# Seven products of quarters instead of eight in the second MLP product of a streaming encoder layer

## The chip, the cores and the metric

The kernel runs on one core of one Trainium2 chip. The metric is the device time of one execution in microseconds (us), the median over runs. The core has a matrix engine (PE, with its own row PEld for the loading of stationary operands), a vector engine (DVE), an activation engine (ACT), a general engine (POOL) and a queue that issues transfers (SP). Each works through its own list of instructions in order and waits on semaphores for the others.

## The reference

One layer with two sub-layers, 512 tokens of 1024 features, all in float32. The first is a mixer (sparse attention with a top-k selection of keys, beside a convolution module), the second the squared-ReLU MLP that the change is about:

```python
x = x + gt1 * (mixed @ w_out[l])
h2 = rms_norm(x, g_norm2[l]) * (1.0 + sc2) + sh2
f = jnp.square(jax.nn.relu(h2 @ w_ff1[l])) @ w_ff2[l]      # w_ff1: 1024 x 4096, w_ff2: 4096 x 1024
x = x + gt2 * f
```

## The kernel before

**Products in three passes.** Every float32 product is made of three matmuls on operands split into a rounded high part and the rest: high times high, high times low, low times high (`mm3`). A weight tile of 128 x 512 therefore takes a cast on ACT (`wh_...`, the high part) and a subtraction (`wl_...`, the low part) on DVE or POOL; the table `ENG` names the engine for each pair of tiles (`P` for POOL, `V` for DVE). The tiles `wh` and `wl` live in rings of four buffers each, so at most four weight tiles stand ahead of PE.

**The MLP in blocks.** The 4096 hidden features are cut into four blocks of 1024 (`NB`). For one block, `ff1` makes two groups of 512 hidden features (first product, hidden features on the partitions, tokens along the moving side), applies ReLU and square on ACT, and splits the result `f` (high part by a DVE cast, low part by a POOL subtraction). `ff2` multiplies them with the block's rows of `w_ff2` (second product, 128 tokens per bank, 512 output columns) in two column halves `n` and adds the banks `y...` to an accumulator `facc` in SBUF.

**Three phases.** `PHASES` says which tokens a block is done for. `A` blocks do the first 256 tokens (`fA`, `yA`) as soon as these are through the mixer; `F` blocks do all 512 tokens (`fF`, `yF`); `B` blocks at the end do the last 256 tokens (`fB`, `yB`) for the blocks that `A` did. With `NA = 2`, blocks 0 and 1 go through `A` and `B`, and blocks 2 and 3 through `F`. In `A` and `B` the first product has a moving side of 256 tokens, in `F` of 512. After the last but one contribution the accumulator is multiplied by the gate `gt2` and added to the residual `x` on POOL; the last contribution is gated and added on DVE and stored.

**What sets the order.** All operations are recorded, and a list scheduler in the kernel (`_Plan`) places them engine by engine. An operation's urgency comes from the numbers in the table `URG`; buffers from rings are given out while it plans. All instructions are issued by one helper line, L433 in the profile of this kernel (L436 after the change), so rows are told apart by tile names. `blk` tiles are sixteen buffers of 128 x 2048 words for everything large.

The names after the change: `q...` is a quarter of the block's part of `w_ff2` (512 rows by 512 columns), `t1` a stored combination of quarters, `p1` to `p7` the seven products (two banks each), `lh`/`ll` the high and low part of a left operand (256 tokens by 512 hidden features, in two steps), `u` a partial sum that two output quarters share.

Of the kernel before, what the change touches and what calls it, by code (L numbers as in the profile page):

```python
# [18 lines left out]
P = 128  # L19
# [11 lines left out]
NEG_MASK = -1.0e30  # L31
FILLER = False
URG = dict(
    ahead_c1=837.59, ahead_iq=272.3, warm=546.0, g0=-393.95, gr=-25.32, w72=-132.21, ps72=260.94,
    start=-1047.26, glu=36.26, c0=-607.51, ik=-47.66, iq=-114.09, iqn=547.0, idx=-2.2, rel=-14.62, topk=612.37,
    c1=602.08, q=132.4, qn=717.77, k=161.16, kn=23.37, qT=215.6, v=238.29, vn=144.89, kT=270.05, tapV0=-394.95,
    tapV1=-965.11, tapV2=584.84, tapV3=12.43, tapP0=202.52, tapP1=412.49, tapP2=412.6, tapP3=-1042.96,
    sh2=117.75, sc2=780.82, gt1=-341.13, gt2=-105.75, gemv_step=23.900000000000006, ahead_x=-11.51,
    ahead=150.51, cn=119.17, pyc=38.83, oC=531.98, attn=-1100.76, sm=-209.79999999999995, pv=-37.5,
    sq=-103.80000000000004, oA=415.94, n2=537.09, ff=543.09, tapVs=33.89999999999999, tapPs=25.450000000000003,  # L40
    topks=18.800000000000004, idxs=5.0, ns=24.0, projs=6.749999999999996, cns=17.89999999999999, oCs=-0.5,
    attns=13.850000000000001, topkB=1479.47, qTB=611.37, attnB=177.79, oB=574.12, n2B=543.32,
)
ENG = dict(
    sl0B="P", sl1B="V", oAmul0="P", oAmul1="P", oAadd0="V", oAadd1="P", oBmul0="V", oBmul1="V", oBadd0="V",
    oBadd1="V", gt1="T", gt2="V", round0="T", round1="T", round2="T", round3="T", sl0="A", sl1="P", rope_q="P",
    rope_k="P", rope_iq="P", gb="P", oAadd="P", oCmul="A", oAmul="V", lo_c0="V", lo_c1="V", lo_iq="P", lo_q="P",
    lo_k="P", lo_v="P", lo_oC="P", lo_oA="P", lo_oB="P", lo_f1A="PPVV", lo_f2A="PVVV", lo_f1F="VPPP",
    lo_f2F="PVPP", lo_f1B="PVPV", lo_f2B="VVVP", h2lo0="V", h2lo1="V", aff0="A", aff1="A", mixA="P", tap0="A",
)  # L50
POOL_TAPS = (7, 7, 11, 12)
NB = 4
NA = 2
NBLK = 16
PHASES = (("A", range(NA)), ("F", range(NA, NB)), ("B", range(NA)))


# [456 lines left out]
def layer_kernel(  # L514
# [52 lines left out]
    def blk(shape, dt, name):  # L567
        return big.tile(shape, dt, tag="B", bufs=NBLK, name=name)

# [14 lines left out]
    def raw(ap):  # L584
        return ap.bitcast(F32)
# [690 lines left out]
    def x2(t):  # L1276
        return x2s[t // 2][:, t % 2, :]
# [213 lines left out]
    facc = [blk([P, 2, D], F32, f"facc{half}") for half in range(2)]  # L1491
    count = [0, 0]

    def ff1(b, g, part):
        c0 = b * 1024 + g * 512
        name = f"f{part}{b}{g}"
        hi, lo = dict(A=h2a, B=h2b, F=h2)[part]
        width = S if part == "F" else 256
        banks = [acc_bank(f"{name}_{j}") for j in range(4)]
        for k in (0, 2, 4, 6):  # L1500
            e = dict(P=pl.gpsimd, V=pl.vector)[ENG[f"lo_f1{part}"][k // 2]]
            w = split_weights(rows2(w_ff1, k, c0), f"{name}{k}", e)
            feat_major(banks, w, k, 2, hi, lo, k == 0, k == KD - 2, width)
        if part == "F":
            f = [blk([P, 4, S], F32R, f"{name}{a}") for a in range(2)]
            for j in range(4):
                r = tmp_tile(f"r{name}{j}")
                pl.scalar.activation(r, banks[j], AF.Relu)
                pl.scalar.activation(r, r, AF.Square)
                pl.vector.tensor_copy(f[0][:, j, :], r)  # L1510
                pl.gpsimd.tensor_sub(f[1][:, j, :], r, raw(f[0][:, j, :]))
            return f
        f = blk([P, 2, 4, 256], F32R, name)
        for j in (0, 2):
            r = tmp_tile(f"r{name}{j}").rearrange("p (j q) -> p j q", j=2)
            for jj in range(2):
                pl.scalar.activation(r[:, jj, :], banks[j + jj][:, :256], AF.Relu)
            pl.scalar.activation(r, r, AF.Square)
            pl.vector.tensor_copy(f[:, 0, j : j + 2, :], r)
            pl.gpsimd.tensor_sub(f[:, 1, j : j + 2, :], r, raw(f[:, 0, j : j + 2, :]))  # L1520
        return [f[:, 0], f[:, 1]]

    def ff2(b, n, part, fts):
        c0 = n * 512
        tiles = dict(A=(0, 1), B=(2, 3), F=(0, 1, 2, 3))[part]
        banks = {t: wk_bank(f"y{part}{b}{n}_{t}") for t in tiles}
        for k in (0, 2, 4, 6):
            e = dict(P=pl.gpsimd, V=pl.vector)[ENG[f"lo_f2{part}"][k // 2]]
            w = split_weights(rows2(w_ff2, b * 8 + k, c0), f"y{part}{b}{n}{k}", e)
            f = fts[k // 4]  # L1530
            for t in tiles:
                i = t if part == "F" else t % 2
                s = slice(i * P, (i + 1) * P)
                for kk in range(2):
                    j = k % 4 + kk
                    mm3(banks[t], (f[0][:, j, s], f[1][:, j, s]), w[kk], k + kk == 0, k + kk == 7)
        for t in tiles:
            a = facc[t // 2][:, t % 2, c0 : c0 + 512]
            xs = x2(t)[:, c0 : c0 + 512]
            g = gt2[:, c0 : c0 + 512]  # L1540
            m = count[t // 2]
            if m == 0:
                pl.scalar.copy(a, banks[t])
            elif m < NB - 1:
                pl.vector.tensor_add(a, banks[t], a)
            else:
                pl.vector.tensor_mul(a, banks[t], g)
                pl.vector.tensor_add(a, a, xs)
                pl.sync.dma_start(out[t * P : (t + 1) * P, c0 : c0 + 512], a)
            if m == NB - 2:  # L1550
                pl.gpsimd.tensor_mul(a, a, g)
                pl.gpsimd.tensor_add(xs, xs, a)

    for part, blocks in PHASES:
        for b in blocks:
            fts = []
            for g in range(2):
                step += 1
                pl.level = (URG["ff"] + 20 * step,)
                fts.append(ff1(b, g, part))  # L1560
            for n in range(2):
                step += 1
                pl.level = (URG["ff"] + 20 * step,)
                ff2(b, n, part, fts)
            for h in dict(A=(0,), B=(1,), F=(0, 1))[part]:
                count[h] += 1
# [53 lines left out]
```

## Time and profile before

| | us |
|---|---|
| median of 3 runs (lowest, highest) | 665.84 (665.34, 665.88) |
| the profiled execution | 665.98 |
| its span, first to last instruction | 664.1 |
| PE busy | 639.7 (96%) |
| DVE busy | 402.8 (61%) |
| POOL busy | 393.7 (59%) |
| ACT busy | 347.7 (52%) |

1.9 us of the profiled execution lie outside its span. Busy shares are means over stages with different limits; the stages in the trace are: mixer to 299 us, `A` blocks 298.9 to 394.8, `F` blocks 394.8 to 568.9, `B` blocks from 568.9 to the end. A matmul's recorded duration overlaps that of its neighbours, so the pace of a stream of them is taken from a stretch of time divided by their count. The same holds for DVE: what counts in a row of operations is the distance from start to start.

### The profile page before, as it was taken

How to read it: one execution, taken by the hardware profiler on the slowest of the kernel's cores; microseconds unless marked ns; L12 is line 12 of the kernel's file. 1: busy time of each engine (PE TensorE's matmuls, PEld its weight loads, DVE VectorE, ACT ScalarE, POOL GpSimd, SP SyncE). 2: the span in 40 equal slices, each digit the busy share in tenths (PEclk: the TensorE clock that was granted, in tenths of full speed). 3: DMA queues.
4: the chain of work that ended last, by engine and by line, in shares of the span. 5: the costliest groups of instructions: out<-in, count | busy, mean ns of one | idle time of the engine just before them, and what ended most of it. 6: DMA issues, size and time to landing. Idle time of an engine off the chain costs nothing. (4 is left out here: it accounts for less than half of the span.)

```text
span 664.1 us, 10353 instructions
## 1 busy us (share of the span) xinstructions
PE 639.7 (96%) x3654; PEld 523.0 (79%) x3654; DVE 402.8 (61%) x812; ACT 347.7 (52%) x711; POOL 393.7 (59%) x379
## 2 busy tenths in 40 slices
PE   3999999999998999999999999999999999999997
PEld 2776776878675776679989988888888888998985
DVE  4657999999999899987752641122102220465564
ACT  3327625894359855976656533342225422464552
POOL 2008936999999789633445523766466643448941
PEclk9999999999999899999999999999999999999999
DMA  9969995423031264107565563232322334555552
GB/s 292 348 207 388 368 387 198 162 64 96 33 95 36 94 221 127 32 17 224 177 200 178 190 191 112 80 96 95 125 86 84 118 85 137 159 183 179 185 186 94
DMA packets 61662, 105.09 MB, mean 158 GB/s; under 512 B 6233, under 2 KB 22825, under 8 KB 61610
## 3 DMA queue, kind: packets, MB, share of 16 engines
q1 hardware_dynamic: 61514, 104.39, 48.2%
q8 instruction: 29, 0.48, 0.3%
q14 instruction: 23, 0.19, 0.1%
q10 hardware_dynamic: 96, 0.03, 0.0%
HBM read 100.22 MB, written 2.10 MB: 154 GB/s over the span
## 5 line engine op out<-in xcount | busy, mean ns | idle before, releaser
L433 PE MATMUL yF<-wh_yF,fF 128*128 128x512 f32 x256 | 79.2, 389 | 0.0
L433 PE MATMUL fF<-h,wh_fF 128*128 128x512 f32 x256 | 78.8, 389 | 0.0
L433 DVE SCALAR_TENSOR_TENSOR run<-u,wdw,run 128x512 f32<-128x512 f32 x83 | 58.9, 748 | 0.2
L433 PEld LDWEIGHTS yF<-wh_yF,fF 128*128 128x128 f32 x256 | 48.0, 188 | 10.1
L433 PEld LDWEIGHTS fF<-h,wh_fF 128*128 128x128 f32 x256 | 48.0, 188 | 10.0
L433 POOL TENSOR_TENSOR wl_yF<-wr_yF,wh_yF 128x512 fp32r<-128x512 f32 x24 | 30.5, 1291 | 35.5 <-ACT wh_yF L433 35.5
L433 PE MATMUL fF<-h,wl_fF 128*128 128x512 f32 x128 | 49.8, 389 | 0.0
L433 PE MATMUL yF<-wl_yF,fF 128*128 128x512 f32 x128 | 49.8, 389 | 0.0
L433 ACT CAST wh_yF<-wr_yF 128x512 fp32r<-128x512 f32 x32 | 19.9, 622 | 51.5 <-PE yF L433 38.6
L433 PE MATMUL fA<-h2a,wh_fA 128*128 128x256 f32 x256 | 46.5, 284 | 0.0
L433 POOL TENSOR_TENSOR cacc<-cacc,prod 128x512 f32<-128x512 f32 x33 | 44.0, 1336 | 3.7 <-ACT prod L433 2.9
L433 POOL TENSOR_TENSOR wl_fF<-wr_fF,wh_fF 128x512 fp32r<-128x512 f32 x24 | 31.3, 1324 | 24.8 <-ACT wh_fF L433 22.1
L433 PE MATMUL fB<-h,wh_fB 128*128 128x256 f32 x256 | 45.4, 283 | 0.0
L433 ACT CAST wh_fF<-wr_fF 128x512 fp32r<-128x512 f32 x32 | 19.9, 622 | 45.4 <-PE fF L433 37.5
L433 PEld LDWEIGHTS fA<-h2a,wh_fA 128*128 128x128 f32 x256 | 40.0, 191 | 0.3
L433 PE MATMUL yA<-wh_yA,fA 128*128 128x512 f32 x128 | 39.7, 389 | 0.0
L433 PE MATMUL yB<-wh_yB,fB 128*128 128x512 f32 x128 | 39.6, 390 | 0.0
L433 PEld LDWEIGHTS fB<-h,wh_fB 128*128 128x128 f32 x256 | 39.5, 192 | 0.2
L433 PE MATMUL fA<-h2a,wl_fA 128*128 128x256 f32 x128 | 35.7, 283 | 0.0
L433 PE MATMUL fB<-h,wl_fB 128*128 128x256 f32 x128 | 34.8, 284 | 0.2 <-POOL wl_fB L433 0.2
L433 DVE CAST fF<-rfF 128x512 fp32r<-128x512 f32 x16 | 8.2, 523 | 43.9 <-ACT rfF L433 43.9
L433 DVE TENSOR_TENSOR wl_fF<-wr_fF,wh_fF 128x512 fp32r<-128x512 f32 x8 | 5.5, 693 | 48.1 <-ACT wh_fF L433 48.1
(328 smaller groups left out, 1845.4 us busy)
## 6 DMA issues: line engine op xcount, KB each, us to landing
wa_gt<-in_w_ada_dram SPq DMA_DIRECT2D x16, 512.0 KB, 9.4
wr_fA<-in_w_ff_dram SPq DMA_DIRECT2D x16, 512.0 KB, 4.1
wr_yA<-in_w_ff_dram SPq DMA_DIRECT2D x16, 512.0 KB, 3.8
wr_fF<-in_w_ff_dram SPq DMA_DIRECT2D x16, 512.0 KB, 3.8
wr_yF<-in_w_ff_dram SPq DMA_DIRECT2D x16, 512.0 KB, 3.6
wr_fB<-in_w_ff_dram SPq DMA_DIRECT2D x16, 512.0 KB, 4.1
wr_yB<-in_w_ff_dram SPq DMA_DIRECT2D x16, 512.0 KB, 3.7
ada<-in_w_ada_dram SPq DMA_DIRECT2D x12, 512.0 KB, 8.4
```

The costliest lines, as they stand in the source:

```text
L433: f(*map(real, args), **{k: real(v) for k, v in kwargs.items()})
```

## The change

For `F` blocks (`SEVEN = "F"`) the second product is done by quarters. The left side `f` (512 tokens by 1024 hidden features) and the right side (1024 by 1024) are each cut into two by two quarters, and seven products of sums and differences of quarters replace the eight plain ones. The sums of left quarters (`fsum`) are done in place on DVE, the sums of weight quarters (`wsum`) on DVE for three tiles of four and on POOL for one; `f` is kept in plain float32, and each of the seven left operands is split anew (high part on ACT, low part on DVE), as is each of the 28 weight tiles (high part on ACT, low part on DVE). Products that two output quarters share are added to both.

`NA` goes from 2 to 1: block 0 alone goes through `A` and `B`, blocks 1, 2 and 3 through `F`. Both tables are new. One more convolution tap is done by ACT and POOL in place of DVE (`POOL_TAPS`). In `B`, all low parts and the split of `f` go to DVE, and so do the gating and the addition to the residual ahead of the last contribution (`foldF`).

```diff
-    lo_k="P", lo_v="P", lo_oC="P", lo_oA="P", lo_oB="P", lo_f1A="PPVV", lo_f2A="PVVV", lo_f1F="VPPP",
-    lo_f2F="PVPP", lo_f1B="PVPV", lo_f2B="VVVP", h2lo0="V", h2lo1="V", aff0="A", aff1="A", mixA="P", tap0="A",
+    lo_k="P", lo_v="P", lo_oC="P", lo_oA="P", lo_oB="P", lo_f1A="PPVP", lo_f2A="PVPV", lo_f1F="PVPP",
+    lo_f2F="VVVP", lo_f1B="VVVV", lo_f2B="VVVV", sumF="VPVV", losF="VVVV", fsumF="V", fhiF="A", floF="V",
+    uaddF="V", foldF="V", frest="V", h2lo0="V", h2lo1="V", aff0="A", aff1="A", mixA="P", tap0="A",
 )
-POOL_TAPS = (7, 7, 11, 12)
+POOL_TAPS = (7, 8, 11, 12)
 NB = 4
-NA = 2
+NA = 1
+SEVEN = "F"
...
-    def ff1(b, g, part):
+    def ff1(b, g, part, pair=None):
...
+        if part in SEVEN:
+            f = blk([P, 4, S], F32, name) if part == "F" else pair[:, g]
+            for j in range(4):
+                pl.scalar.activation(f[:, j, :], banks[j][:, :width], AF.Relu)
+                pl.scalar.activation(f[:, j, :], f[:, j, :], AF.Square)
+            return f
...
-            pl.gpsimd.tensor_sub(f[:, 1, j : j + 2, :], r, raw(f[:, 0, j : j + 2, :]))
+            eng("frest").tensor_sub(f[:, 1, j : j + 2, :], r, raw(f[:, 0, j : j + 2, :]))
...
+    def evict(bank, t, n, m, last):
+        c0 = n * 512
+        a = facc[t // 2][:, t % 2, c0 : c0 + 512]
+        xs = x2(t)[:, c0 : c0 + 512]
+        g = gt2[:, c0 : c0 + 512]
+        if m == NB - 1 and last:
+            pl.vector.tensor_mul(a, bank, g)
+            pl.vector.tensor_add(a, a, xs)
+            pl.sync.dma_start(out[t * P : (t + 1) * P, c0 : c0 + 512], a)
+            return
+        if (t, n) not in begun:
+            pl.scalar.copy(a, bank)
+        elif bank.tile.psum:
+            pl.vector.tensor_add(a, bank, a)
+        else:
+            eng("uaddF").tensor_add(a, bank, a)
+        begun.add((t, n))
...
+    def ff2_seven(b, part, f, lev_load, start):
...
+        a11, a21 = (f[0][:, :, r * half : (r + 1) * half] for r in range(2))
+        a12, a22 = (f[1][:, :, r * half : (r + 1) * half] for r in range(2))
+        quarters = []
+        with pl.after([start]), pl.urgency(lev_load):
+            for g, n in ((0, 0), (0, 1), (1, 1), (1, 0)):
+                q = blk([P, 4, 512], F32, f"q{part}{b}{g}{n}")
+                for k in (0, 2):
+                    pl.sync.dma_start(q[:, k : k + 2, :], rows2(w_ff2, b * 8 + 4 * g + k, n * 512))
+                quarters.append(q)
+        b11, b12, b22, b21 = quarters
...
+        def product(name, l, r):
+            banks = [wk_bank(f"{name}{part}{b}_{i}") for i in range(half // P)]
+            level = pl.level[0]
+            with pl.urgency(level - URG["ahead"]):
+                ls = left(l, f"{name}{part}{b}")
+            for k in range(4):
+                with pl.urgency(level - URG["ahead"]):
+                    w = right(r, k, f"{name}{part}{b}")
+                for i, bank in enumerate(banks):
+                    s = slice(i * P, (i + 1) * P)
+                    mm3(bank, (ls[k][0][:, s], ls[k][1][:, s]), w, k == 0, k == 3)
+            return banks
...
+        for k in range(4):
+            wsum("tensor_sub", k, t1, b12, b11)
+        for k in range(4):
+            wsum("tensor_sub", k, b12, b22, b12)
+        p = product("p1", a11, b11)      # copied to u (ACT), added to output quarter 1,1
+        fsum("tensor_sub", a11, a11, a21)
+        p = product("p7", a11, b12)      # added to quarters 2,2 and 2,1
+        wsum("tensor_add", k, b11, b11, b12)
+        p = product("p2", a12, b21)      # added to quarter 1,1
+        fsum("tensor_sub", a11, a22, a11)
+        p = product("p6", a11, b11)      # added to u, and u to quarter 2,1
+        wsum("tensor_sub", k, b12, b21, b11)
+        p = product("p4", a22, b12)      # added to quarter 2,1
+        fsum("tensor_add", a21, a21, a22)
+        p = product("p5", a21, t1)       # added to u, and u to quarters 2,2 and 1,2
+        fsum("tensor_sub", a11, a12, a11)
+        p = product("p3", a11, b22)      # added to quarter 1,2
```

(The last part is shortened: levels, loops over `k` and the additions are told in words after the `#`.)

The order that the scheduler makes of it, at three places. In the names, the digits after `F` or `B` count the block, and after it the weight tile: `wl_p2F22` is the low part of the third weight tile of product `p2` in block 2, `yF30_1` the bank of tokens 128 to 255, column half 0, in block 3.

**PE, second product of an all-token block.** Before (block 3), each bank gets its matmuls tile by tile, the three passes of a tile together (`fF300` and `fF301` are the high and low part of `f`):

```order
L433 MATMUL yF30_0_5661<-wh_yF3000_5608,fF300_5474 128x512
L433 MATMUL yF30_0_5661<-wl_yF3000_5613,fF300_5474 128x512
L433 MATMUL yF30_0_5661<-wh_yF3000_5608,fF301_5480 128x512
L433 MATMUL yF30_0_5661<-wh_yF3001_5615,fF300_5474 128x512
L433 MATMUL yF30_0_5661<-wl_yF3001_5623,fF300_5474 128x512
L433 MATMUL yF30_0_5661<-wh_yF3001_5615,fF301_5480 128x512
```

After (block 2, products `p2` and `p6`):

```order
L436 MATMUL p2F2_1_5400<-wh_p2F21_5372,llp2F20_5362 128x512
L436 MATMUL p2F2_0_5390<-wh_p2F22_5383,lhp2F22_5366 128x512
L436 MATMUL p2F2_1_5400<-wh_p2F22_5383,lhp2F22_5366 128x512
L436 MATMUL p6F2_0_5422<-wh_p6F20_5407,lhp6F20_5393 128x512
L436 MATMUL p2F2_0_5390<-wl_p2F22_5413,lhp2F22_5366 128x512
L436 MATMUL p2F2_0_5390<-wh_p2F22_5383,llp2F22_5376 128x512
L436 MATMUL p2F2_1_5400<-wl_p2F22_5413,lhp2F22_5366 128x512
L436 MATMUL p2F2_1_5400<-wh_p2F22_5383,llp2F22_5376 128x512
```

The passes that need only high parts, one of them of the next product, have moved ahead of those with the low part `wl_p2F22`.

**DVE, second product of an all-token block.** Before (block 3), two low parts, two casts of `f` and the first sum out of a bank stand in a row, and this is most of what DVE has in half of a second product:

```order
L433 TENSOR_TENSOR wl_yF3020_5663<-wr_yF302_5531,wh_yF3020_5655 128x512
L433 TENSOR_TENSOR wl_yF3021_5674<-wr_yF302_5531,wh_yF3021_5667 128x512
L433 CAST fF310_5636<-rfF312_5651 128x512
L433 CAST fF310_5636<-rfF313_5671 128x512
L433 TENSOR_TENSOR facc0_4128<-yF30_0_5661,gt2_968 128x512
L433 TENSOR_TENSOR facc0_4128<-facc0_4128,x20_2963 128x512
```

After (block 2, from `p6` to `p4`):

```order
L436 TENSOR_TENSOR llp6F22_5439<-fF20_5086,lhp6F22_5428 128x512
L436 TENSOR_TENSOR facc0_4106<-p2F2_0_5390,facc0_4106 128x512
L436 TENSOR_TENSOR facc0_4106<-p2F2_1_5400,facc0_4106 128x512
L436 TENSOR_TENSOR wl_p6F21_5456<-qF200_4951,wh_p6F21_5420 128x512
L436 TENSOR_TENSOR wl_p6F22_5462<-qF200_4951,wh_p6F22_5436 128x512
L436 TENSOR_TENSOR wl_p6F23_5466<-qF200_4951,wh_p6F23_5452 128x512
L436 TENSOR_TENSOR qF201_4961<-qF210_4984,qF200_4951 128x512 x2
L436 TENSOR_TENSOR llp4F20_5480<-fF21_5252,lhp4F20_5446 128x512
L436 TENSOR_TENSOR wl_p4F20_5489<-qF201_4961,wh_p4F20_5460 128x512
L436 TENSOR_TENSOR uF2_0_5331<-p6F2_0_5422,uF2_0_5331 128x512
```

The low parts of the weights of two products are now mixed with sums out of banks, sums of weight quarters (`qF201`), splits of left operands (`ll`) and partial sums (`uF2`), without a break.

**DVE, start of the B block.** Before, after the sums out of the last `yF` banks:

```order
L433 TENSOR_TENSOR facc1_5185<-yF31_2_5838,facc1_5185 128x512
L433 TENSOR_TENSOR facc1_5185<-yF31_3_5845,facc1_5185 128x512
L433 TENSOR_TENSOR wl_fB0020_5975<-wr_fB002_5834,wh_fB0020_5960 128x512
L433 TENSOR_TENSOR wl_fB0021_5982<-wr_fB002_5834,wh_fB0021_5968 128x512
L433 TENSOR_TENSOR wl_fB0060_6043<-wr_fB006_5908,wh_fB0060_6031 128x512
L433 TENSOR_TENSOR wl_fB0061_6050<-wr_fB006_5908,wh_fB0061_6040 128x512
```

After:

```order
L436 TENSOR_TENSOR wl_fB0000_6346<-wr_fB000_5807,wh_fB0000_6335 128x512
L436 TENSOR_TENSOR facc1_4677<-uF3_0_6042,facc1_4677 128x512
L436 TENSOR_TENSOR wl_fB0001_6356<-wr_fB000_5807,wh_fB0001_6349 128x512
L436 TENSOR_TENSOR facc1_4677<-uF3_1_6053,facc1_4677 128x512
L436 TENSOR_TENSOR wl_fB0020_6368<-wr_fB002_5850,wh_fB0020_6360 128x512
L436 TENSOR_TENSOR facc0_4106<-uF3_0_6042,facc0_4106 128x512
L436 TENSOR_TENSOR facc0_4106<-uF3_1_6053,facc0_4106 128x512
L436 TENSOR_TENSOR wl_fB0021_6391<-wr_fB002_5850,wh_fB0021_6375 128x512
L436 TENSOR_TENSOR x20_2959<-x20_2959,facc0_4106 128x512
L436 TENSOR_TENSOR facc0_4106<-p2F3_1_6111,gt2_960 128x512
```

The low parts of the B block's first weights are mixed with the sums and gatings that the last block of seven products leaves behind.

More of the change, by code (lines that the diff above doesn't have):

```diff
@@ L33 @@
 URG = dict(
[L34 to L42, printed above, removed]
+    ahead_c1=1124.25, ahead_iq=270.95, warm=-302.25, g0=-2.77, gr=-946.01, w72=-374.86, ps72=142.64,
@@ new lines @@
+    start=-1336.17, glu=220.87, c0=-516.25, ik=-128.98, iq=-203.0, iqn=802.64, idx=-944.18, rel=-72.55,
+    topk=217.54, c1=807.1, q=89.88, qn=475.39, k=121.19, kn=-274.6, qT=191.77, v=220.03, vn=-196.25, kT=57.55,
+    tapV0=-112.18, tapV1=-903.31, tapV2=532.94, tapV3=-44.08, tapP0=20.16, tapP1=709.96, tapP2=-50.45,
+    tapP3=-907.8, sh2=71.07, sc2=1160.76, gt1=-376.43, gt2=-91.51, gemv_step=14.099999999999998, ahead_x=40.59,
+    ahead=106.98, cn=131.33, pyc=-292.14, oC=416.69, attn=-947.53, sm=-318.99999999999983,
@@ L43 @@
+    pv=-17.900000000000034, sq=-106.10000000000007, oA=368.14, n2=542.37, ff=604.64, tapVs=30.900000000000002,
+    tapPs=80.45000000000006, topks=17.30000000000001, idxs=8.65, ns=27.050000000000008, projs=6.999999999999994,
+    cns=29.400000000000027, oCs=-0.2, evict=475.23, usum=80.52, attns=32.800000000000054, topkB=1787.89,
+    qTB=389.63, attnB=230.88, oB=621.61, n2B=662.17,
 )
 ENG = dict(
-    sl0B="P", sl1B="V", oAmul0="P", oAmul1="P", oAadd0="V", oAadd1="P", oBmul0="V", oBmul1="V", oBadd0="V",
+    sl0B="P", sl1B="V", oAmul0="V", oAmul1="P", oAadd0="P", oAadd1="P", oBmul0="V", oBmul1="P", oBadd0="P",
@@ L1492, in layer_kernel @@
     count = [0, 0]
-    def ff1(b, g, part):
+    seven_last = [h for h, part in enumerate("FB") if part in SEVEN]
+    begun = set()
+    def ff1(b, g, part, pair=None):
         c0 = b * 1024 + g * 512
@@ L1552, in ff2 @@
                 pl.gpsimd.tensor_add(xs, xs, a)
+    def evict(bank, t, n, m, last):
[14 more added lines that the diff above has]
+            eng("uaddF").tensor_add(a, bank, a)
+        begun.add((t, n))
@@ L1556, in layer_kernel @@
             fts = []
+            pair = blk([P, 2, 4, 256], F32, f"f{part}{b}") if part in SEVEN and part != "F" else None
+            mark = len(pl.ops)
             for g in range(2):
@@ L1559, in layer_kernel @@
                 pl.level = (URG["ff"] + 20 * step,)
-                fts.append(ff1(b, g, part))
+                fts.append(ff1(b, g, part, pair))
+            start = next(op for op in pl.ops[mark:] if op.engine == "tensor")
+            if part in SEVEN:
+                lev_load = pl.level[0] - 20
+                step += 1
+                pl.level = (URG["ff"] + 20 * step,)
+                step += 1
+                ff2_seven(b, part, fts, lev_load, start)
+                for h in dict(A=(0,), B=(1,), F=(0, 1))[part]:
+                    count[h] += 1
+                continue
             for n in range(2):
```

85 lines of the change are left out of this document (added).

## Prediction

> **What bounds the kernel now.** I read the page's busy shares and slices first, then busy times by stage, then the matmul pace, then the rows of DVE, the engine that gets the new work.
>
> ```profile
> span 664.1 us, 10353 instructions
> PE 639.7 (96%) x3654; PEld 523.0 (79%) x3654; DVE 402.8 (61%) x812; ACT 347.7 (52%) x711; POOL 393.7 (59%) x379
> PE   3999999999998999999999999999999999999997
> DVE  4657999999999899987752641122102220465564
> ```
>
> PE is full from the second slice on; DVE is full until slice 17 (282 us) and nearly idle in slices 25 to 34. The same by stage (busy us of PE, PEld, DVE, ACT, POOL, with counts; then clock, transfers):
>
> ```profile
> 195.00:250.00 55.00, 50.85 (x262) 38.35 (x261) 50.96 (x158) 44.74 (x131) 47.09 (x57) 0.97 0.33 106
> 250.00:299.00 49.00, 45.99 (x260) 34.04 (x259) 44.84 (x121) 36.69 (x101) 31.30 (x34) 1.00 0.19 60
> 325.00:395.00 70.00, 70.00 (x415) 62.51 (x415) 36.58 (x48) 42.03 (x81) 30.18 (x22) 1.00 0.60 188
> 395.00:482.00 87.00, 87.00 (x385) 72.03 (x385) 15.39 (x21) 30.53 (x52) 49.47 (x39) 1.00 0.33 103
> 482.00:569.00 87.00, 87.00 (x386) 72.03 (x385) 16.65 (x25) 29.39 (x50) 45.71 (x36) 1.00 0.32 99
> 438.40:482.00 43.60, 43.60 (x194) 36.12 (x193) 9.96 (x12) 13.03 (x23) 24.75 (x20) 1.00 0.32 100
> ```
>
> From 325 to 569 us PE has no gap at all: it alone sets that stage, and what it is spared there is gained, as long as the others keep up. DVE does 12 operations in a second product (last row). Mixer stages lose 4.15 and 3.01 us of PE, together 7.2.
>
> **The change part by part.** *Fewer matmuls.* Two rows: the 512-wide matmuls of one `F` block, and a stretch of a `B` block's first product, 256 wide.
>
> ```profile
> 395.00:482.00 87.00, 86.95 (x384) 72.03 (x385) 4.10 (x8) 4.77 (x8) 10.30 (x8) 1.00 0.33 103
> 569.00:592.00 23.00, 23.00 (x193) 22.96 (x192) 9.88 (x14) 12.83 (x26) 10.19 (x8) 1.00 0.59 192
> ```
>
> A 512-wide matmul costs 86.95/384 = 0.2264 us, a 256-wide one 23.00/193 = 0.119. A second product falls from 192 matmuls to 7 x 24 = 168, in three blocks: 72 x 0.2264 = 16.3 us. Block 1 goes from two halves (2 x 192 x 0.119 = 45.8) to one `F` product (192 x 0.2264 = 43.5): 2.3 us; its second product in halves has as many matmuls as whole. PE is spared **18.6 us**. The same block also loads its 16 weight pieces once instead of twice, worth nothing, since no PE wait on them shows above.
>
> *What DVE gets.* Counted in the order, from the third weight tile of `p1` (the first that must wait for `ff1` to release a buffer) to the last tile of `p3`, DVE has 58, 59 and 65 operations in the three blocks: 26 low parts of weights, 11 of left operands, 4 sums of left and 5 of weight quarters, 12 to 14 sums out of banks or of `u`, and in the last block 5 gatings and final additions. PE takes 168 x 0.2264 = 38.0 us for this. All are 128 x 512; the rows that price them:
>
> ```profile
> 319.91 1.28 DVE L433 TENSOR_TENSOR wl_fA<-wr_fA,wh_fA 128x512 fp32r<-128x512 f32 x2
> 321.11 1.28 DVE L433 TENSOR_TENSOR x<-x,xr 128x512 f32<-128x512 f32 x2
> 322.32 1.28 DVE L433 TENSOR_TENSOR wl_fA<-wr_fA,wh_fA 128x512 fp32r<-128x512 f32 x2
> 647.33 0.69 DVE L433 TENSOR_TENSOR facc<-yB,gt 128x512 f32<-128x512 f32 x1
> 648.06 0.69 DVE L433 TENSOR_TENSOR facc<-facc,x 128x512 f32<-128x512 f32 x1
> 648.69 0.69 DVE L433 TENSOR_TENSOR facc<-yB,gt 128x512 f32<-128x512 f32 x1
> 649.30 1.29 DVE L433 TENSOR_TENSOR wl_yB<-wr_yB,wh_yB 128x512 fp32r<-128x512 f32 x2
> ```
>
> Each is recorded with 0.69 us, but they start closer: two every 1.20 to 1.21 (0.60 each) when independent, 0.61 to 0.63 beside a bank, 0.73 where one needs the one just before. With five to seven of the last kind among some 60 I take **0.62** on average, with 0.60 and 0.69 as ends.
>
> Such an operation is late when 0.7 us (the cast on ACT ahead of the first) plus 0.62 x its place exceeds the time at which PE comes to it. Seven products are 5.43 us each, one weight tile 1.36. In block 1 the latest is the second tile of `p3`, place 56: 0.7 + 34.7 against 6 x 5.43 + 1.36 = 33.9, late by 1.5. In block 2 it is the second tile of `p4`, place 40: 25.5 against 23.1, late by 2.4. In block 3, again the second tile of `p3`, place 63: 39.8 against 33.9, late by 5.9. Whatever is late is PE time, since PE's list holds the next block's matmuls only behind `p3`. Sum **9.8** (at 0.60: 0.4 + 1.6 + 4.6 = 6.6; at 0.69, where block 2 is latest at place 57: 5.4 + 6.1 + 10.3 = 21.8). What is queued behind on DVE is the next tiles' low parts, which is why lateness carries over from product to product.
>
> In the `B` block all low parts are DVE's now, behind sums and gatings: the second tile of the seventh pair has place 33 after the last tile of `p3`, so 20.5 us against 1.36 + 6 x 24 x 0.119 + 3 x 0.119 = 18.9: late by **1.6** (0.9 to 3.9).
>
> *POOL beside DVE.* One sum of weight quarters of four stays on POOL. What a POOL operation does to DVE:
>
> ```profile
> 595.21 2.38 DVE L433 TENSOR_TENSOR wl_yB<-wr_yB,wh_yB 128x512 fp32r<-128x512 f32 x2
> 595.36 1.67 POOL L433 TENSOR_TENSOR fB<-rfB,fB 128x512 fp32r<-128x512 f32 x1 [1.56 <-DVE fB L433]
> ```
>
> Two operations take 2.38 instead of 1.28 when one of POOL's falls between: 1.1 us. Within a second product POOL has two; the first falls where DVE waits for ACT anyway, the second (`b12` during `p7`) where DVE has no slack. So 1.1 per block, **3.3** in all (0 if it falls in a gap, 6.6 if both count).
>
> *ACT.* Per second product 28 casts of weights and 14 of left operands. Two casts take 1.30 us, 0.69 apart:
>
> ```profile
> 645.29 1.30 ACT L433 CAST wh_yB<-wr_yB 128x512 fp32r<-128x512 f32 x2 [1.42 <-PE yB L433]
> ```
>
> 42 x 0.69 = 29, and with copies to `u` and the last squares of `ff1` some 33 of 38 us: it fits, and costs nothing by itself. If ACT slipped, DVE's low parts would be late next, by the same amount.
>
> *Transfers.* Quarters come in 8 pieces of 512 KB per block, as before, but are released only when the block's first matmul starts. That lets SP hold later pieces of `w_ff1` behind them; a piece lands in 3.6 to 3.8 us and the pieces behind are needed over 27 us later (half of 43.5 plus 5.4), so nothing:
>
> ```profile
> wr_fF<-in_w_ff_dram SPq DMA_DIRECT2D x16, 512.0 KB, 3.8
> wr_yF<-in_w_ff_dram SPq DMA_DIRECT2D x16, 512.0 KB, 3.6
> ```
>
> *One block ahead, not two.* `F` needs the second half's normalised tokens. When these are ready, and when `F` starts:
>
> ```profile
> L433 DVE TENSOR_TENSOR h<-ht,h x4: 692/694/1668, 309.4 to 330.9; 128x512 fp32r<-128x512 f32 x4
> L433 PE MATMUL fF<-h,wh_fF x256: 389/389/389, 395.0 to 525.2; 128*128 128x512 f32 x128
> ```
>
> Ready at 331.6. `F` moves forward by one `A` block, 192 x 0.119 + 96 x 0.2264 = 44.6 us, to 350.4. That leaves 18.8 us of cover: nothing. If it were gone, PE would wait for these tokens microsecond for microsecond.
>
> *The mixer's new order and the tap taken from DVE.* The same matmuls, another order. The bounds are the 7.2 us of gaps above: at best they close, at worst they grow by about half, 3. I take 0, as no row prefers a side.
>
> The sum: -18.6 + 9.8 + 1.6 + 3.3 = **-3.9**. The profiled execution took 665.98 (1.9 outside its span, 0.1 over the median of 665.84), so **662.1 us**.
>
> VectorE: DVE Perf Modes, a page of the Trainium skill, says under "The DRAIN you can't avoid" that the next DVE operation starts only once the pipe has emptied behind the one before. If that meant a full 0.69 us for each, the sum would come to the slower side. The trace does not bear it out for independent operations: six in a row start 0.60 apart.
>
> **The rivals.** (1) *DVE takes its full recorded time*, because its operations wait one by one for casts, banks or their predecessors. For it: 0.73 between dependent ones, and the order alternates such kinds. Against: runs at 0.60. At 0.69 the lateness is 21.8 + 3.9 + 3.3 = 29.0 against 18.6 saved: 665.98 + 10.4 = **676**, and without the clashes with POOL 673. It decides the sign from a mean distance of about 0.64 on, since each 0.01 is worth some 2 us (places 56, 57, 63 and 33) and 3.9 are to be lost. (2) *DVE keeps up*: the sums fall into gaps and PE never waits. Against: 36 to 41 us of DVE work must end within some 37. It gives 665.98 - 18.6 = **647.4**. (3) *The cover is missed*: the mixer's second half comes over 18.8 us later in the new order, by 7 us beyond that, say, as much as PE lost there in all, and PE waits at the start of `F`: 662.1 + 7 = **669**. Against: DVE has a tap less to do and the order of the mixer's matmuls is nearly unchanged.
>
> **How the numbers follow.** Chances: forecast 0.60, rival 1 0.19, rival 2 0.13, rival 3 0.08. The forecast's own range, from 0.60 without clashes (665.98 - 18.6 + 6.6 + 0.9 = 654.9) to 0.65 with them (6 us more than at 0.62), is 655 to 668. Bounds for 8 in 10: below, most of rival 2 is left out and the mixer's gain is taken in, 652; above, half of rival 1 is let in, 672. A measurement of this kernel can tell 0.2%, 1.3 us, from no change: 664.5 to 667.2. The forecast lies below it with 0.78, in it with 0.14, above with 0.08; rival 2 is faster, rivals 1 and 3 slower with 0.9 and same otherwise. Faster: 0.47 + 0.13 = 0.60; same 0.08 + 0.03 = 0.11; slower 0.05 + 0.24 = 0.29.
>
> **What would show it.** Right: some 18 us less between first and last matmul if PE's waits are taken off; PE busy in the `ff1` stretches and 2.5 to 7 us of waits per second product, on `wl_p...` from DVE, growing from block 1 to 3, the longest ahead of `p3`; DVE over 90% busy there and near 50% in `ff1`; `fF` first at about 350. Wrong: PE waits of 6 us and more in each second product (rival 1), none (rival 2), or a gap ahead of the first `fF` on `h` (rival 3); or PE waiting for ACT's casts, which I cost at nothing.

## The result, and the profile after

The changed kernel takes **653.71 us** (median of 4 runs, 653.18 to 654.25), the kernel before 665.59 beside it: a ratio of 0.9827 with a 95% interval of 0.9807 to 0.9847. It is faster by 11.9 us where I had forecast 3.9. The profiled execution took 653.37 us, 651.6 of them in its span. First the page: span, busy shares, and the slices of PE and DVE.

```profile
span 651.6 us, 9935 instructions
PE 624.4 (96%) x3390; PEld 500.3 (77%) x3390; DVE 510.3 (78%) x995; ACT 376.1 (58%) x756; POOL 306.5 (47%) x308
PE   4999999999999899989999999999999999998997
DVE  3657999999999899998553628975289942899995
```

PE has 15 us less to do and DVE 107 us more, and the DVE row now shows three humps of eights and nines at the end where it had ones and zeros: the three second products. Their stretches, from the first matmul of `p1` to the first of what follows `p3` (busy us of PE, PEld, DVE, ACT, POOL, with counts; then clock and transfers), and behind them the `B` block:

```profile
394.33:432.48 38.15, 38.15 (x169) 31.45 (x168) 36.95 (x62) 27.22 (x48) 4.89 (x3) 1.00 0.01 1
476.54:515.97 39.43, 39.01 (x170) 31.22 (x168) 39.04 (x64) 25.50 (x44) 4.54 (x3) 1.00 0.00 1
559.49:601.97 42.48, 39.26 (x169) 31.21 (x168) 42.15 (x71) 25.25 (x44) 1.62 (x1) 1.00 0.02 7
602.00:647.00 45.00, 44.95 (x289) 40.84 (x287) 39.11 (x66) 22.19 (x41) 0.00 (x0) 1.00 0.53 170
```

168 matmuls at 0.2264 us are 38.04 us. So PE is late by 0.1, 1.4 and 4.4 us in the three products, 5.9 together, and not at all in the `B` block. DVE is busy for 97 to 99% of each product. What PE waits for there, in the whole stretch:

```profile
PE p5F L436 <- DVE facc L436: 2.1, 1, 2.1
PE p4F L436 <- DVE uF L436: 0.7, 1, 0.7
PE p3F L436 <- DVE wl_p3F L436: 0.3, 1, 0.3
PE p4F L436 <- DVE wl_p4F L436: 0.3, 1, 0.3
PE fF L436 <- POOL wl_fF L436: 0.2, 1, 0.2
```

All but the last wait for DVE, and the two long ones are in block 3: `p4` and `p5` wait until DVE has emptied a bank (`u` out of `p6`, `facc` out of `p4`), because it keeps the two banks of `p2` for the final gating that stands late in its list (it empties them at 593.3 and 604.8). The wait that ends last there is still one on DVE's list: the second low part of `p3` is done at 598.15, with DVE working up to it with a single pause of 0.23 us, and PE, held up for the last time, starts on it at 598.21:

```profile
598.21 0.50 PE L436 MATMUL p3F<-wl_p3F,lhp3F 128*128 128x512 f32 x1 [0.27 <-DVE wl_p3F L436]
```

The second half's tokens, whose cover I had put at 18.8 us, and the first `F` block:

```profile
L436 DVE TENSOR_TENSOR h<-ht,h x4: 680/693/1668, 331.0 to 344.6; 128x512 fp32r<-128x512 f32 x4
L436 PE MATMUL fF<-h,wh_fF x384: 387/389/402, 350.8 to 559.0; 128*128 128x512 f32 x192
```

`F` starts at 350.8 (forecast 350.4), and the tokens are ready at 345.3. They came 13.7 us later than before, so the cover is down to 5.5 us: it held, with far less to spare than I had counted. What delayed them in the mixer stays open.

### The profile page after: what moved, and what is told of

Same layout as the page of the kernel before. It is cut to its first block, busy times and chain, and to the rows that moved or that the text cites. A ratio compares the mean times of both kernels' runs of the same rounds, so it can differ in the third digit from the quotient of the medians.

```text
span 651.6 us, 9935 instructions
## 1 busy us (share of the span) xinstructions
PE 624.4 (96%) x3390; PEld 500.3 (77%) x3390; DVE 510.3 (78%) x995; ACT 376.1 (58%) x756; POOL 306.5 (47%) x308
## 3 DMA queue, kind: packets, MB, share of 16 engines
q1 hardware_dynamic: 57162, 96.00, 44.6%
## 5 line engine op out<-in xcount | busy, mean ns | idle before, releaser
L436 PE MATMUL fF<-h,wh_fF 128*128 128x512 f32 x384 | 118.3, 389 | 0.0
L436 PE MATMUL fF<-h,wl_fF 128*128 128x512 f32 x192 | 74.8, 390 | 0.2 <-POOL wl_fF L436 0.2
L436 PEld LDWEIGHTS fF<-h,wl_fF 128*128 128x128 f32 x192 | 36.0, 188 | 8.1 <-POOL wl_fF L436 0.6
L436 ACT ACTIVATE fF<-fF 128x512 f32<-128x512 f32 x48 | 29.1, 613 | 6.9 <-PE fF L436 5.5
L436 PE MATMUL c<-hTlo,wh_c 128*128 128x512 f32 x64 | 26.0, 407 | 0.8 <-DVE hTlo L436 0.8
L436 DVE MATCH_REPLACE8 sc<-m,sc 128x256 f32<-128x256 f32 (+2 forms) x48 | 25.7, 539 | 0.0
L436 DVE TENSOR_TENSOR qF<-qF,qF 128x512 f32<-128x512 f32 x27 | 25.4, 963 | 0.4
L436 PE MATMUL c<-hThi,wl_c 128*128 128x512 f32 x64 | 25.4, 397 | 0.0
L436 DVE MAX8 m<-sc 128x8 f32<-128x256 f32 (+2 forms) x48 | 25.0, 543 | 0.0
L436 PE MATMUL c<-hThi,wh_c 128*128 128x512 f32 x64 | 24.3, 400 | 0.5 <-ACT hThi L436 0.4
```

Source lines behind the costliest of these rows:

```text
L436: f(*map(real, args), **{k: real(v) for k, v in kwargs.items()})
```

## The experiments

Each edit is to the changed kernel unless it says otherwise. "Late" is the time from the first matmul of `p1` to the first one behind `p3`, less 38.04 us. Times are medians; ratios, with 95% intervals, are to the kernel before timed beside each run, whose own times went from 663 to 674 us.

**The two parts apart.** First the changed kernel without the seven products:

```diff
-SEVEN = "F"
+SEVEN = ""
```

> The changed kernel with all second products as eight products of whole blocks (no Strassen), but with one block ahead for the first half and the changed order. Theory A (the gain is matmuls spared, less what DVE is late): the three second products have 72 matmuls more, 72 x 0.2264 = 16.3 us, and lose the 5.8 us that PE waits in them now, so 653.4 + 16.3 - 5.8 = 663.9 us, and no wait of PE between the first matmul of the first F block and the end of the last. Rival B (much of the gain is the changed order of the mixer and of the transfers): about 657 us or less.

663.24 us (ratio 0.9922, 0.9893 to 0.9952): theory A, to 0.7 us. The six products in a row have no gap of PE:

```profile
350.46:611.58 261.12, 261.12 (x1154) 216.29 (x1153) 67.87 (x97) 89.43 (x150) 106.44 (x84) 1.00 0.33 103
```

The same stretch takes 251.16 us with the seven products (350.81 to 601.97): 9.96 less, which is the 16.3 of matmuls less 5.9 of lateness and 0.5 in the `ff1` behind block 1. Fewer half-blocks and the new order make the span 661.3 us instead of 664.1, which is the 2.3 us of the forecast and a little more; the seven products bring the rest. Then the other part alone:

```diff
-NA = 1
+NA = 2
```

> The changed kernel with two blocks, not one, ahead for the first half of the tokens, so that only blocks 2 and 3 are F blocks with seven products. Theory A: two second products spare 48 x 0.2264 = 10.9 us and PE is late by about 0 in the first and 4.3 us in the second, which has the final additions; 665.98 - 10.9 + 4.3 = 659.4 us. Rival B (the lateness comes with the third product of seven in a row, as the queues of DVE and ACT fall behind from block to block): the second one waits under 2 us, so about 657 us.

660.17 us (0.9886, 0.9842 to 0.9929), theory A again. Its two second products:

```profile
439.24:477.39 38.15, 38.15 (x169) 31.46 (x168) 36.95 (x62) 27.22 (x48) 4.88 (x3) 1.00 0.00 1
521.45:563.91 42.46, 39.22 (x169) 31.23 (x168) 42.14 (x71) 25.26 (x44) 1.63 (x1) 1.00 0.02 7
```

They are 0.1 and 4.4 late, the same as blocks 1 and 3 of three. Lateness does not pile up from block to block; it belongs to what each block gives DVE to do.

**Is it DVE's list?** Fourteen operations taken from it per second product:

```diff
-                eng(f"flo{part}").tensor_sub(lo, v, raw(hi))
+                pl.scalar.copy(lo, v)
```

> Left out: the low parts of the left operands are not computed; ACT copies the left operand in their place, so DVE has 14 operations fewer per second product and ACT 14 more (0.69 us each: 25 + 9.7 of 38 us). Matmuls as before. Theory A (what PE waits for is DVE's list): the latest operation of block 2 is in time, that of block 3 comes 1.7 us late instead of 4.3; 653.4 - 5.8 + 1.7 = 649 us. Rival B (PE's waits come from the chain bank to sum to next product, or from ACT, whatever the length of DVE's list): 653 us or more, with waits of PE for ACT's casts.

649.79 us (0.9726, 0.9683 to 0.9768); the last product, with DVE at 39.5 us and ACT at 30.5:

```profile
558.61:598.41 39.80, 39.21 (x169) 31.23 (x168) 39.52 (x66) 30.46 (x55) 1.30 (x1) 1.00 0.04 14
```

Late by 0.3, 0.5 and 1.8: what PE waited for was DVE's list, and ACT had room for fourteen operations more.

**Does POOL's sum cost DVE 1.1 us?** All sums on DVE:

```diff
-sumF="VPVV"
+sumF="VVVV"
```

> All sums of weight quarters on DVE, none on POOL. Theory A (DVE's list is the bound, at one operation per 0.61 us, and POOL's one sum beside it costs DVE nothing): counted in the order, the operation that PE waits for longest moves from place 40 to 41 or so in block 2 and from 63 to 67 in block 3; 1.4 and 2.4 us later, so 653.4 + 3.8 = 657 us. Theory B (POOL's sum costs DVE 1.1 us per block, as I forecast): those 3.3 us come back, so 653.4 + 3.8 - 3.3 = 654 us.

659.15 us (0.9871, 0.9832 to 0.9910). Taking POOL out makes it slower, so theory B falls: in the changed kernel there was nothing to get back. But theory A is 2 us short. Block by block it is late by 0.5, 2.8 and 7.2. In block 3 PE waits 3.93 us ahead of `p5`, and then its matmuls are slow; PE's timeline behind that wait, and the stretch:

```profile
594.39 0.77 PE L436 MATMUL p5F<-wh_p5F,lhp5F 128*128 128x512 f32 x1 [3.93 <-DVE facc L436]
594.96 0.63 PE L436 MATMUL p5F<-wl_p5F,lhp5F 128*128 128x512 f32 x1
595.38 0.63 PE L436 MATMUL p5F<-wh_p5F,llp5F 128*128 128x512 f32 x1
...
598.35 0.39 PE L436 MATMUL p5F<-wl_p5F,lhp5F 128*128 128x512 f32 x1
598.58 0.39 PE L436 MATMUL p5F<-wh_p5F,llp5F 128*128 128x512 f32 x1
```

```profile
594.40:597.00 2.60, 2.60 (x6) 2.11 (x7) 2.57 (x5) 0.00 (x0) 0.00 (x0) 0.50 0.00 0
```

They start 0.43 us apart instead of 0.227, at a granted clock of 0.50, for some 3.3 us. `p5` takes 7.16 us instead of 5.44: 1.7 us on top of the wait, most of the 2 that were missing.

Then POOL given more, in four ways. One low part of four:

```diff
-losF="VVVV"
+losF="VVVP"
```

> One low part of four in every product goes from DVE to POOL: seven POOL operations per second product, where the changed kernel has one. Theory A (POOL's operations cost DVE nothing there): DVE's list is 7 to 13 operations shorter at the latest place, block 1 and 2 are in time and block 3 is 2.5 us late, so 653.5 - 5.8 + 2.5 = 650 us. Theory B (an operation of POOL on SBUF holds DVE up by some 1.1 us, as between the two low parts of the B block before; the changed kernel escapes it only because POOL's one sum falls beside DVE's two sums out of banks): each operation moved costs DVE 1.1 and saves it 0.61, 7 x 0.5 = 3.4 us per block, three blocks, so about 664 us.

All sums of weight quarters:

```diff
-sumF="VPVV"
+sumF="PPPP"
```

> All sums of weight quarters on POOL, 16 per block, of which about 8 fall into the products. Theory A (POOL costs DVE nothing): the latest place of DVE is 57 in block 3, 0.6 us late, and in time before; 653.5 - 5.8 + 0.6 = 648 us. Theory B (1.1 us of DVE per operation of POOL): 8 x 1.1 - 6 x 0.61 = 5 us per block more on DVE's list, about 666 us; or PE waits for POOL's sums themselves, 1.3 to 1.7 us each and four in a row.

The additions of `u`:

```diff
-uaddF="V"
+uaddF="P"
```

> The six additions of u to the output sums per second product go from DVE to POOL (12 on POOL in all where the block has them late, some beside p3 and the next ff1). Theory A: DVE's latest places are 56, 58 and 23, 0, 1.3 and 0.2 us late, so 653.5 - 5.8 + 1.5 = 649 us. Theory B (1.1 us of DVE per operation of POOL on SBUF): the additions come late in the list, four of the six ahead of or beside p3, 4 x (1.1 - 0.61) = 2 us in blocks 1 and 2 and somewhat less in block 3: 653 to 656 us.

Three sums of four and the gating:

```diff
-sumF="VPVV"
-foldF="V"
+sumF="VPPP"
+foldF="P"
```

> Three sums of weight quarters of four on POOL and the gating of finished sums (mul, add) in the last block too. Theory A: latest place of DVE 57 of 58, 1.1 us late in block 3 and in time before, so 653.5 - 5.8 + 1.1 = 649 us. Theory B (1.1 us of DVE per operation of POOL): 6 more operations of POOL in each second product, 3 us per block, and 12 in the last: about 663 us.

They took 671.29, 664.02, 661.39 and 670.52 us (ratios 1.0062, 1.0031 to 1.0092; 0.9947, 0.9910 to 0.9984; 0.9922, 0.9890 to 0.9953; 1.0051, 1.0018 to 1.0084). Theory A missed by 12 to 22 us; theory B has the right side throughout and is 7 to 8 us short in the first and the last, 5 in the third, and 2 over in the second. The mechanism, in the kernel with POOL's low parts (DVE, then POOL; behind them the stretch of its last product):

```profile
412.65 2.37 DVE L436 TENSOR_TENSOR wl_p6F<-qF,wh_p6F 128x512 fp32r<-128x512 f32 x2
412.20 1.68 POOL L436 TENSOR_TENSOR wl_p6F<-qF,wh_p6F 128x512 fp32r<-128x512 f32 x1 [2.27 <-DVE facc L436]
```

```profile
570.55:619.82 49.27, 42.74 (x169) 32.91 (x168) 45.81 (x67) 25.50 (x44) 12.84 (x8) 0.93 0.03 11
```

Two operations take 2.37 us instead of 1.28. The products are late by 5.3, 8.6 and 11.2, and the clock is down to 0.93: part of what theory B lacked is again the slow matmuls behind a long wait. In the kernel with POOL's additions the loss up to there fits theory B's 653 to 656: the `B` block's first product has its last matmul at 626.5 us, against 624.9 in the changed kernel, 1.6 later. The rest of its loss lies in the `B` block's second product, which theory B did not count: 1.3 and 1.9 us shortly one after the other ahead of `yB`, and then

```profile
632.00:636.00 4.00, 4.00 (x11) 3.03 (x11) 3.58 (x8) 1.24 (x2) 0.00 (x0) 0.50 0.28 108
```

half the clock through these 4 us. In the four profiles, in the order above, the clock stands at 0.50 behind such waits for 10.2, 10.2, 6.8 and 13.6 us. By an estimate from half of these lengths the clock costs at most 5.1, 5.1, 3.4 and 6.8 us. With that taken off, theory B is 1 to 2 us short in three of the four, and 7 over in the kernel with all sums on POOL. That fits the spread of this kernel's own runs: 658.16 us at a mean clock of 0.999, 667.76 at 0.982. So theory B has the right side and roughly the right size for three kernels; why all sums on POOL cost less than it says stays open.

**Why POOL's one sum is free where it stands.** In block 2 of the changed kernel it starts at 481.83; DVE's rows around it:

```profile
481.83 1.62 POOL L436 TENSOR_TENSOR qF<-qF,qF 128x512 f32<-128x512 f32 x1 [7.35 <-issue]
481.62 0.69 DVE L436 TENSOR_TENSOR fF<-fF,fF 128x512 f32<-128x512 f32 x1
482.22 0.68 DVE L436 TENSOR_TENSOR facc<-p1F,facc 128x512 f32<-128x512 f32 x1
483.12 0.69 DVE L436 TENSOR_TENSOR facc<-p1F,facc 128x512 f32<-128x512 f32 x1 [0.22 <-ACT uF L436]
```

DVE keeps its distance; POOL's sum takes 1.62 instead of 1.29, so it is POOL that waited, for the operation on `fF`, and then ran beside the two sums that read a bank. To move it, I first shifted the sum by one part:

```diff
-sumF="VPVV"
+sumF="VVPV"
```

> POOL's sum of weight quarters is the third of four, not the second: as many operations on each engine, but POOL's falls behind the third low part of p7, beside DVE's operations on SBUF, not beside the two sums out of the banks of p1. Theory A (POOL's one operation costs DVE nothing wherever it stands): by the order DVE's latest places make 0.6 us more, 654.3 us. Theory B (it costs 1.1 us wherever DVE works on SBUF and escapes beside the two bank sums only): 1.1 us more in blocks 2 and 3 and up to that in block 1, so 656 to 657.5 us.

660.49 us (0.9893, 0.9844 to 0.9943), past theory B. But this moved other things too. POOL's sum during `p1` now meets a low part (1.57 us instead of 0.69), while the one during `p7` falls where DVE waits for ACT:

```profile
477.21 1.29 POOL L436 TENSOR_TENSOR qF<-qF,qF 128x512 f32<-128x512 f32 x1 [9.13 <-DVE wl_p1F L436]
477.48 1.57 DVE L436 TENSOR_TENSOR wl_p1F<-qF,wh_p1F 128x512 fp32r<-128x512 f32 x1 [0.35 <-ACT wh_p1F L436]
483.84 0.69 DVE L436 TENSOR_TENSOR facc<-p1F,facc 128x512 f32<-128x512 f32 x1 [1.06 <-ACT uF L436]
```

With a longer wait for `u`, and in block 3 a 4.87 us wait ahead of `p5` and 6.8 us of half clock around its end, this run does not settle the place of the operation. The next ones do; they start from a better version.

**The gating out of the products.** Of the finished sums of block 3 nothing is gated until the `B` block:

```diff
         if m == NB - 1 and last:
-            pl.vector.tensor_mul(a, bank, g)
-            pl.vector.tensor_add(a, a, xs)
-            pl.sync.dma_start(out[t * P : (t + 1) * P, c0 : c0 + 512], a)
+            pl.vector.tensor_add(a, bank, a)
+            with pl.urgency(pl.level[0] + 650):
+                pl.vector.tensor_mul(a, a, g)
+                pl.vector.tensor_add(a, a, xs)
+                pl.sync.dma_start(out[t * P : (t + 1) * P, c0 : c0 + 512], a)
...
-                if number(t) == NB - 1 and more == 1 or number(t) == NB - 2 and not more and t // 2 not in seven_last:
-                    fold(t, n)
+                if number(t) == NB - 2 and not more and t // 2 not in seven_last:
+                    with pl.urgency(pl.level[0] + 100):
+                        fold(t, n)
```

> The changed kernel itself once more, beside the other two of this group on one chip: 653.7 us as before, within 0.2% or 1.3 us, with PE late by 0, 1.4 and 4.4 us in the three second products.

> The finished sums of the last F block are first added up like the others and gated later, beside the B block, instead of being gated within the products (same results, four operations of DVE fewer in all, five fewer ahead of the place that PE waits for). Theory A (block 3 is later than block 2 only by these operations on DVE's list): the latest place falls from 63 to 40, the same as in block 2, so PE is late by 1.4 us instead of 4.4 there: 653.7 - 3.0 = 650.7 us, and the waits of PE ahead of p4 on u and ahead of p5 on facc are gone. Rival (the lateness adds up from block to block, whatever the operations): 653.7 us.

On one chip the changed kernel took 654.30 us (0.9803, 0.9754 to 0.9852) and this version 651.47 (0.9762, 0.9709 to 0.9815): 2.8 less, 3.0 expected. Block 3 is now as late as block 2, 1.4 us, and the waits on `u` and `facc` are gone (the banks of `p2` are emptied at 576.3 and 576.9):

```profile
559.49:598.93 39.44, 39.05 (x169) 31.24 (x168) 39.04 (x66) 25.54 (x44) 1.63 (x1) 1.00 0.00 1
```

In the new profile of the changed kernel PE is late by 0.1, 1.4 and 5.9 us, not 0.1, 1.4 and 4.4: the last section comes back to this.

**POOL's second sum, beside SBUF and beside banks.** On top of that, the third part of the sum ahead of `p4` goes to POOL. In three kernels: with a one-column copy that is to hold the sum back until DVE has begun on `p7`'s banks, without the copy, and with copy and sum tied together so that nothing comes between them. The edit of the third (the first has no `pl.block()`, the second neither that nor the copy):

```diff
-                wsum("tensor_sub", k, b12, b21, b11)
+                if k == 2:
+                    mark = tmp.tile([P, 1], F32, tag="mark", name=f"mark{part}{b}", bufs=2)
+                    with pl.block():
+                        pl.gpsimd.tensor_copy(mark, facc[1][:, 0, 512:513])
+                        pl.gpsimd.tensor_sub(b12[:, k, :], b21[:, k, :], b11[:, k, :])
+                else:
+                    wsum("tensor_sub", k, b12, b21, b11)
```

> From the version that gates late (651.5 us): one more sum of weight quarters per block goes to POOL (the third part of the sum ahead of p4), and a one-column copy ahead of it makes POOL wait for DVE's first sum out of p7's banks, so that it runs beside the three that follow. Theory A (POOL beside DVE's bank sums costs DVE nothing): DVE's latest place in blocks 2 and 3 is 39 instead of 40, each 0.6 us earlier: 651.5 - 1.2 = 650.3 us, and every DVE operation there starts 0.60 us behind the one before. Theory B (any operation of POOL costs DVE 1.1 us): 651.5 + 2 x 0.5 to 3 x 1.1, 652.5 to 654.8 us.

> The same without the one-column copy: POOL may begin its second sum as soon as p7's third low part is made, while DVE works on SBUF operands one behind the other; DVE's list in the products is the same, word for word. Theory A1 (whoever is working keeps the other out, and DVE without a pause keeps POOL out until its next bank sum): as with the copy, 650.3 us, with POOL's sum recorded longer. Theory A2 (POOL gets in between two operations of DVE on SBUF and holds the second up by 1.1 us): 1.1 us more in each of three blocks, less the slack of block 1, 652.5 to 653.6 us.

651.97 (0.9775, 0.9733 to 0.9817) and 652.69 us (0.9783, 0.9737 to 0.9829). The copy missed its aim: it came to stand behind the sum on POOL's list, so both kernels show the same, theory A2 (POOL and DVE, the kernel without the copy, block 2):

```profile
485.55 1.62 POOL L436 TENSOR_TENSOR qF<-qF,qF 128x512 f32<-128x512 f32 x1 [1.09 <-DVE wl_p7F L436]
485.94 2.38 DVE L436 TENSOR_TENSOR llp2F<-fF,lhp2F 128x512 fp32r<-128x512 f32 x2
```

2.38 instead of 1.28: 1.1 us. Both kernels are late by 0.6, 1.9 and 1.9 us. With copy and sum tied together:

> As in the two runs before (one more sum per block on POOL, on top of gating late), but the one-column copy now stands right ahead of that sum on POOL, so the sum begins behind DVE's first sum out of p7's banks and runs beside the three that follow. Theory A (an operation of POOL costs DVE 1.1 us beside operands on SBUF and nothing beside bank sums): all of DVE's operations start 0.60 us behind the one before in all three blocks, the 1.1 us per block are gone, PE is late by 0.5 to 0.8 us in blocks 2 and 3; 650.3 us. Theory B (it costs 1.1 us wherever DVE is busy): as in the two runs before, 652 to 652.7 us, with one pair of DVE operations at 2.4 us in each block.

650.67 us (0.9752, 0.9711 to 0.9793), theory A. POOL's sum runs at its full pace and so do DVE's four beside it, in block 2, whose whole stretch stands behind them:

```profile
489.21 1.30 POOL L436 TENSOR_TENSOR qF<-qF,qF 128x512 f32<-128x512 f32 x1
488.33 2.48 DVE L436 TENSOR_TENSOR facc<-p7F,facc 128x512 f32<-128x512 f32 x4
```

```profile
476.92:515.83 38.91, 38.75 (x170) 31.37 (x168) 38.51 (x63) 25.57 (x44) 5.88 (x5) 1.00 0.01 1
```

Late by 0.5, 0.9 and 0.9, so 1.0 less in blocks 2 and 3 than without the tie. The scheduler also put a few of DVE's operations in another order there; the rows, more than the times, show what POOL's sum costs. It is the shortest median of the kernels that compute all of the result, 15.0 us below the 665.68 of the kernel before beside it, and some 3 below the changed kernel, though that was timed in other groups; against the version that only gates late the 0.8 us lies within what the runs scatter.

## Why the prediction was right or wrong

The mechanism was right: PE is spared what was counted, DVE's list takes part of it back, most in the block with the final additions, and the first `F` block stands where it was put. The gain was forecast at a third of its size because three terms of the sum, all charged against the change, were too large: DVE's lateness in the products by 3.9, POOL by 3.3, the `B` block by 1.6. Term by term, in us:

| term | forecast | profile after |
|---|---|---|
| PE spared | -18.6 | -18.6 (the run without the seven products confirms both parts) |
| DVE late in the three products | 1.5 + 2.4 + 5.9 = 9.8 | 0.1 + 1.4 + 4.4 = 5.9 |
| DVE late in the `B` block | 1.6 | 0 |
| POOL beside DVE | 3.3 | 0 |
| mixer's order | 0 | 0.4 (`F` at 350.8, not 350.4) |
| ACT, transfers, other low parts | 0 | 0.5 (`ff1` behind block 1 takes 44.0 us, not 43.5) |
| sum | -3.9 | -11.8; the profiled executions differ by 12.6 |

Of the 0.8 that the sum lacks, 0.4 lies in the last `B` block, which takes 45.0 us from its first matmul to its last before and 44.6 after; I did not trace the rest.

**The term of DVE's lateness (9.8) was 3.9 too large.** The step was "0.7 + 0.62 x place". Block 3 of the changed kernel, the first low part that waits for a buffer (place 1) and the three of `p3` that begin with place 63:

```profile
559.49 0.69 DVE L436 TENSOR_TENSOR wl_p1F<-qF,wh_p1F 128x512 fp32r<-128x512 f32 x1
...
597.47 1.89 DVE L436 TENSOR_TENSOR wl_p3F<-qF,wh_p3F 128x512 fp32r<-128x512 f32 x3
```

The first starts with `p1` itself, at 559.49, so the cast ahead of it was done by then: 0.7 us earlier than I let it. The mean distance is 37.98/62 = 0.613: 0.60 for nearly all, also out of banks, 0.72 two or three times, and one short wait for ACT. And the low part is read in the second of three passes, 0.23 us behind the time I compared with. Together these make 1.4, 1.1 and 1.4 us in the three blocks: 1.5 becomes 0.1, 2.4 becomes 1.3 and 5.9 becomes 4.5. The places themselves, 56, 40 and 63, decided: five fewer operations of gating in block 3 made it as late as block 2. What PE's waits are named after was less good: I said `wl_p...`, and in block 3 it was mostly banks that DVE had not emptied. These waits only take ahead what place 63 costs in any case, since the last one, at 598.21, is on that low part.

**The term of POOL (3.3) was wrong, not its price.** The row of 2.38 us was read rightly: 1.1 us is what a POOL operation costs beside two DVE operations on SBUF, and it came again in three of the runs (2.37 to 2.39). What I left out is where the operation falls. I looked whether DVE had slack there, not what it reads: beside its sums out of banks POOL costs it nothing, which the last runs show: 2.38 us for two operations beside POOL's second sum where it falls on SBUF operands, 2.48 for four where it falls on bank sums, as without it. The Trainium skill has the rule that I should have held against that row, SBUF — State Buffer, "Who interferes with whom": a DVE instruction with two SBUF inputs contends with a GpSimd instruction that reads SBUF, one with at most one SBUF input does not (outside the two-port modes), and whoever starts first keeps the other out. The rows agree in each point: 2.38 against 1.28 with two SBUF inputs, 2.48 for four that each take one from a bank, and 1.62 instead of 1.29 for POOL where DVE was first.

**The term of the `B` block (1.6) came from a wrong starting point.** I let PE reach the last low part of `p3` just as it is made. But PE waits for the second of the four, DVE makes the last three in a row 0.60 apart while PE takes 1.36 for each, and so DVE enters the `B` block some 1.5 us ahead. That is nearly the whole term.

**What I costed at nothing.** ACT had room, as the run with fourteen more copies confirms. The transfers are not seen in PE's waits. The 0.5 us behind block 1 are a consequence of DVE's full list: POOL's first two low parts for the next `ff1`, 2.54 us for such a pair elsewhere, take 4.70 there, beside DVE's last low parts of `p3` and sums of `u`, which have both operands on SBUF; POOL is the one kept out, and PE's first wait in that `ff1` is on its low part.

```profile
429.22 4.70 POOL L436 TENSOR_TENSOR wl_fF<-wr_fF,wh_fF 128x512 fp32r<-128x512 f32 x2 [27.98 <-ACT wh_fF L436]
```

**The rivals.** Rival 1, with 0.69 us per operation, did not come: DVE's distance is 0.60 in some 60 operations per block. The section that I quoted from the Trainium skill (VectorE: DVE Perf Modes, "The DRAIN you can't avoid") also says that a next operation that is not held starts earlier, and these rows agree. Rival 2, no wait at all, gave 647.4 and lies 6.3 us below the result; the forecast lay 8.4 above. Nearer the rival than the forecast, then, though the waits in blocks 2 and 3 were there. Rival 3 was not far off: 13.3 of the 18.8 us of cover were used up, so the new order of the mixer was less alike for this half than I argued against it.

## What to carry to other kernels

When an engine's list is to decide, find the place where it starts to run without a pause, use the distance between starts of independent operations (0.60 here, not the recorded 0.69), and count to the operation that is waited for longest; work that nobody waits for yet, such as a last gating, belongs behind that place. Before an operation goes to POOL, look at what DVE reads beside it: with both operands on SBUF it costs DVE 1.1 us, beside sums out of a bank nothing, and a one-column copy tied to it is enough to put it there. A wait of PE can cost more than its length: here by some 1.5 to 1.7 us, in some executions, after waits of 1.92 to 3.93 us.

## What the runs showed of the hardware

A wait of PE can be followed by half the clock. After the 3.93 us wait above it was 0.50 for 3.3 us, at a cost of 1.7. So it was after a wait of 1.92 us in the kernel with all sums on POOL; the stretch shortly behind it:

```profile
408.29 0.50 PE L436 MATMUL p2F<-wl_p2F,lhp2F 128*128 128x512 f32 x1 [1.92 <-DVE wl_p2F L436]
410.00:412.00 2.00, 2.00 (x6) 1.62 (x5) 1.85 (x4) 0.79 (x2) 0.00 (x0) 0.50 0.00 0
```

The length of the wait alone does not decide. The 2.10 us wait ahead of `p5` in the changed kernel left the clock at 1.00 in all three products. In the second profile of the same kernel the same wait was followed by half clock, and `p5` took 7.13 us; that is what made block 3 late by 5.9 instead of 4.4:

```profile
590.54 0.49 PE L436 MATMUL p5F<-wh_p5F,lhp5F 128*128 128x512 f32 x1 [2.12 <-DVE facc L436]
591.00:594.00 3.00, 3.00 (x9) 2.32 (x8) 2.97 (x5) 0.00 (x0) 0.00 (x0) 0.50 0.00 0
```

And a wait of 2.96 us, in the kernel with three sums and the gating on POOL, left it at 1.00:

```profile
644.78 0.73 PE L436 MATMUL yB<-wh_yB,fB 128*128 128x512 f32 x2 [2.96 <-DVE fB L436]
645.00:652.00 7.00, 7.00 (x32) 5.77 (x32) 4.78 (x9) 2.82 (x5) 0.00 (x0) 1.00 0.63 223
```

The Trainium skill, TensorE: Matmul & The Clock Gate, "What's actually happening", says that the clock is either full or half, by windows of some 3.4 us that run free of the program, and goes down after an idle one. The two values and the 3.3 us agree, and so does a wait that is followed by half clock in one execution and not in another. That a wait of 1.92 us can be enough is more than it says, and fits windows that need not be wholly idle, which no run here tests.
